# The load of the first superblock's gates waits for block 30 of the first expert product

## The chip, the core and the metric

The kernel runs on one core of a Trainium2 chip. The metric is the time of one execution on the device in microseconds (us); the kernel before was timed three times. One further execution was recorded by the profiler, and all rows below come from it. A core has TensorE (PE in the rows, PEld its weight loads), VectorE (DVE), ScalarE (ACT), GpSimd (POOL) and SyncE (SP); each executes its own instructions in order and waits on semaphores for the others.

## The reference

Two transformer blocks over 256 tokens of width 2048, in float32. The part that matters is the expert layer of the second block. Each token picks 16 of 16,384 experts in each of 8 heads; an expert is one row of `peer_u` and one of `peer_v`:

```python
def chunk(args):
    xc, ec, gc = args                     # tokens, chosen experts, their gates
    u = peer_u[ec]
    act = jax.nn.gelu(jnp.einsum('tkd,td->tk', u, xc))
    return jnp.einsum('tk,tkd->td', gc * act, peer_v[ec])
```

The gates are a softmax over the 16 best scores of a head. After this layer a gated projection and a last normalization follow.

## The kernel before

The kernel doesn't gather experts. It computes the layer densely, for all 16,384 of them: a first product of the tokens with all rows of `peer_u`, gelu, a multiply with a gate table that is zero where an expert was not chosen, and a second product with `peer_v`.

The table lies in DRAM as two arrays, `gate_table0` and `gate_table1`, one for each half of the tokens (128 each), experts by tokens. It is filled with zeros early in the program. The routing (`choose`) then adds each gate at its place: 256 indirect DMAs from GpSimd (line 1389, called scatters here), 128 single elements each, half of them into each table. The routing's steps run beside the products of later chunks.

The first product is cut into 32 blocks of 512 experts (`up(eb)`, blocks 0 to 31). A block is a tile of 128 partitions by 4 by 256 tokens. Its weights come in eight loads of 512 KB over SyncE's queue, called chunks here. The helper `wload` splits each chunk into a high part (`wh`, a cast on ScalarE, L217) and a low part (`wl`, a subtraction on VectorE, L218), with five buffers for the raw tiles, four for `wh`, three for `wl`. TensorE multiplies with both (L243 with `wh`, L245 with `wl`). `halves` adds the two accumulators of each bank (a copy on ScalarE, L280, an add on VectorE, L281), and gelu follows on ScalarE (L1421). Blocks 0 to 21 are written to DRAM (`spill`, line 1423); blocks 22 to 31 stay in SBUF in `hsb`.

The second product goes by superblocks of two blocks, first 11 to 15 (blocks 22 to 31, which are at hand), then 0 to 10. `weigh` does three things: it loads the gates into two tiles (line 1435, four loads of 128 x 4 x 128 elements: for each of two blocks one from each table), takes the blocks, and multiplies them with the gates on VectorE (L1445). The blocks are then split into high and low parts again (L301 on ScalarE, L302 on VectorE). `down` multiplies them with `peer_v` (L249 to L251) and adds the result to `hx` (L451). For all superblocks but the first one, `weigh` copies one element of `hx[0]` into the gates' tile ahead of the load (line 1433); the load of the first table overwrites that element and so waits for the copy.

All 32 blocks are called before the first `weigh` in the code. The order in which the instructions of an engine stand is set by a scheduler, which works with the dependences among tiles; the code's order is one of its inputs. The changed lines alone therefore don't tell where an instruction stands.

Of the kernel before, what the change touches and what calls it, by code (L numbers as in the profile page):

```python
# [133 lines left out]
class Kern:  # L134
# [1274 lines left out]
    def experts_(self, hx, xn, n5):  # L1409
        nc, i = self.nc, self.i  # L1410
        self.routing(xn)
        hsb, at = {}, {}
        SPILL, LAG = 11, 5
        spill = self.dramp.tile([2 * SPILL, P, 4, 256], F32, name="spill")
        xt = lambda k: xn.normal[k // 4](k % 4)

        def up(eb):
            banks = self.ws_chunk(xt, lambda kk: i["uT"][eb, kk // 2], KT, 512)
            b4 = self.blk()
            self.halves(b4, banks)  # L1420
            nc.scalar.activation(b4, b4, AF.Gelu_apprx_tanh)  # L1421
            if eb < 2 * SPILL:
                nc.scalar.dma_start(spill[eb], b4)
            else:
                hsb[eb] = b4

        def weigh(sb, first):
            g = []
            for u in range(2):
                gb = self.xp.tile([P, 4, 256], F32, name=self.nm("gates"), tag="gates")  # L1430
                if not first:

                    nc.gpsimd.tensor_copy(gb[:, 0, 0:1], hx[0][:, 0, 0:1])  # L1433
                for t in range(2):
                    nc.gpsimd.dma_start(gb[:, :, P * t:P * t + P], self.gd[t].rearrange("(i p) t -> p i t", p=P)  # L1435
                                        [:, 8 * sb + 4 * u:8 * sb + 4 * u + 4, :])
                g.append(gb)
            ap = []
            for u in range(2):
                if sb < SPILL:  # L1440
                    a = self.blk()
                    nc.gpsimd.dma_start(a, spill[2 * sb + u])
                else:
                    a = hsb.pop(2 * sb + u)
                nc.vector.tensor_tensor(a, a, g[u], OP.mult)  # L1445
                ap.append(Pair(self))
                ap[u].split(a)
            at[sb] = self.tiles_of(ap)

        def down(sb, last):  # L1450
            a = at.pop(sb)
            for j in range(4):
                banks = self.xs_chunk(a, lambda kk: self.wsrc(i["peer_v"], 8 * sb + kk, 512 * j, 512), 8, 512)
                self.add_rows(hx, j, banks)
                if last and j < 3:
                    n5.chunk(j, hx[j])


        order = list(range(SPILL, 16)) + list(range(SPILL))
        for n in range(SPILL + LAG):  # L1460
            up(2 * n)
            up(2 * n + 1)
        self.drain()
        for n, sb in enumerate(order):
            new = SPILL + LAG + n
            if new < 16:
                up(2 * new)
            weigh(sb, n == 0)
            if new < 16:
                up(2 * new + 1)  # L1470
            down(sb, n == 15)
# [195 lines left out]
```

## Time and profile before

| what | value |
|---|---|
| timed runs | 3850.2, 3848.3, 3850.9 us; median 3850.2 |
| profiled execution, device time | 3846.87 us |
| its span, first to last instruction | 3845.1 us |
| mean granted TensorE clock | 0.981 |
| TensorE busy | 3690.7 us (96% of the span) |
| VectorE, ScalarE, GpSimd busy | 63%, 49%, 18% |
| first and last scatter start | 2159.1 and 2827.0 us |
| first and last load of gates start | 2828.4 and 3656.4 us |

The profiled execution's device time lies 1.8 us above its span. In the rows, times are us from the start of the span. A row of a timeline gives start, duration, engine, line and operation, the tiles written and read, and how often it was merged; behind it, in brackets, how long the engine stood idle ahead of it and what released it. The order of an engine's instructions is the program's.

### The profile page before, as it was taken

How to read it: one execution, taken by the hardware profiler on the slowest of the kernel's cores; microseconds unless marked ns; L12 is line 12 of the kernel's file. 1: busy time of each engine (PE TensorE's matmuls, PEld its weight loads, DVE VectorE, ACT ScalarE, POOL GpSimd, SP SyncE). 2: the span in 40 equal slices, each digit the busy share in tenths (PEclk: the TensorE clock that was granted, in tenths of full speed). 3: DMA queues.
4: the chain of work that ended last, by engine and by line, in shares of the span. 5: the costliest groups of instructions: out<-in, count | busy, mean ns of one | idle time of the engine just before them, and what ended most of it. 6: DMA issues, size and time to landing. Idle time of an engine off the chain costs nothing.

```text
span 3845.1 us, 53526 instructions
## 1 busy us (share of the span) xinstructions
PE 3690.7 (96%) x19938; PEld 3163.1 (82%) x19938; DVE 2428.7 (63%) x4232; ACT 1867.3 (49%) x2586; POOL 691.6 (18%) x525
## 2 busy tenths in 40 slices
PE   9999989999999999999999999999249999999998
PEld 8888878888888898888888888888248888888887
DVE  7566667567576775578656998455124566666665
ACT  4344455455455555467645455444124444444455
POOL 0000030000000200001010366678730001111100
PEclk9999999999999999999999999999679999999999
DMA  6534486666666545666665678888346667777765
GB/s 221 150 112 148 137 329 189 195 191 186 195 192 189 163 133 169 194 185 183 179 196 182 182 207 212 211 212 212 48 112 188 200 212 234 249 242 240 237 205 162
DMA packets 368694, 728.82 MB, mean 190 GB/s; under 512 B 61072, under 2 KB 67696, under 8 KB 368432
## 3 DMA queue, kind: packets, MB, share of 16 engines
q1 hardware_dynamic: 311536, 658.19, 56.6%
q0 software_dynamic: 53296, 55.37, 6.4%
q10 hardware_dynamic: 3600, 11.83, 0.8%
q8 instruction: 156, 2.56, 0.3%
q14 instruction: 106, 0.87, 0.1%
HBM read 694.74 MB, written 30.54 MB: 189 GB/s over the span
## 4 chain that ended last, share of the span: by engine, by line
PE 73%; issue 10%; DMA 10%; POOL 4%; DVE 2%; ACT 1%; SPq 0%; DVEq 0%; ACTq 0%; POOLq 0%
PE acc L243 25%; PE acc L245 13%; PE acc L249 10%; PE acc L250 10%; PE acc L251 10%; DMA gate_table<-sm,sm 8%; POOL gate_table L1389 4%; PE ps L479 2%; DMA raw<-in_w_up_dram 1%; DVE wl L218 1%; PE ps L492 1%; DMA raw<-in_w_in_dram 1%; PE ps L1255 0%; PE ps L375 0%; POOL gates L1435 0%
## 5 line engine op out<-in xcount | busy, mean ns | idle before, releaser
L218 DVE TENSOR_TENSOR wl<-raw,wh 128x1024 fp32r<-128x1024 f32 x1249 | 1537.3, 1233 | 984.1 <-PE acc L245 527.1
L217 ACT CAST wh<-raw 128x1024 fp32r<-128x1024 f32 x1249 | 1300.1, 1045 | 1551.9 <-PE acc L243 721.9
L243 PE MATMUL acc<-b,wh 128*128 128x512 f32 x6128 | 1664.1, 397 | 6.6 <-DVE b L281 6.5
L243 PEld LDWEIGHTS acc<-b,wh 128*128 128x128 f32 x6128 | 1061.5, 189 | 163.7 <-DVE b L281 7.9
L245 PEld LDWEIGHTS acc<-b,wl 128*128 128x128 f32 x6128 | 920.4, 190 | 236.5 <-DVE wl L218 119.0
L245 PE MATMUL acc<-b,wl 128*128 128x256 f32 x6128 | 950.4, 282 | 118.2 <-DVE wl L218 118.2
L250 PE MATMUL acc<-wl,b 128*128 128x512 f32 (+1 forms) x1916 | 737.8, 385 | 3.1 <-DVE wl L218 3.0
L249 PE MATMUL acc<-wh,b 128*128 128x512 f32 (+1 forms) x1916 | 738.5, 386 | 0.0
L251 PE MATMUL acc<-wh,b 128*128 128x512 f32 (+1 forms) x1916 | 737.0, 385 | 0.0
L1389 POOL DMA_INDIRECT gate_table<-sm,sm x256 | 475.4, 1857 | 248.6 <-DMA gate_table<-sm,sm 150.0
L250 PEld LDWEIGHTS acc<-wl,b 128*128 128x128 f32 x1916 | 360.4, 188 | 75.6 <-DVE wl L218 6.0
L249 PEld LDWEIGHTS acc<-wh,b 128*128 128x128 f32 x1916 | 360.4, 188 | 74.2 <-issue 4.0
L251 PEld LDWEIGHTS acc<-wh,b 128*128 128x128 f32 x1916 | 360.4, 188 | 70.7 <-DVE b L302 0.3
L280 ACT COPY b<-acc 128x256 f32<-128x256 f32 x398 | 145.6, 371 | 120.1 <-PE acc L245 106.6
L281 DVE TENSOR_TENSOR b<-acc,b 128x256 f32<-128x256 f32 x398 | 164.8, 420 | 42.4 <-ACT b L280 41.3
L451 DVE TENSOR_TENSOR b<-b,acc 128x512 f32<-128x512 f32 x176 | 120.3, 684 | 64.0 <-PE acc L251 63.8
L1445 DVE TENSOR_TENSOR b<-b,gates 128x1024 f32<-128x1024 f32 x32 | 38.8, 1223 | 189.4 <-DMA gates<-gate_table 186.5
L1433 POOL COPY gates<-b 128x1 f32<-128x1 f32 x30 | 18.5, 648 | 750.7 <-DVE b L451 750.7
L954 POOL TENSOR_TENSOR b<-b,b 128x1024 f32<-128x1024 f32 x8 | 19.2, 2406 | 561.7 <-ACT b L953 387.6
L301 ACT CAST b<-b 128x1024 fp32r<-128x1024 f32 (+1 forms) x63 | 58.6, 942 | 125.7 <-DVE b L1445 92.0
L484 ACT ACTIVATE p<-sp,sm 128x128 f32<-128x128 f32 x120 | 53.9, 450 | 74.8 <-DVE sm L483 74.8
L302 DVE TENSOR_TENSOR b<-b,b 128x1024 fp32r<-128x1024 f32 (+1 forms) x63 | 67.9, 1086 | 22.9 <-ACT b L301 22.5
(315 smaller groups left out, 1849.7 us busy)
## 6 DMA issues: line engine op xcount, KB each, us to landing
raw<-in_uT_dram SPq DMA_DIRECT2D x256, 512.0 KB
raw<-in_peer_v_dram SPq DMA_DIRECT2D x256, 512.0 KB
raw<-in_w_in_dram SPq DMA_DIRECT2D x224, 512.0 KB
raw<-in_w_up_dram SPq DMA_DIRECT2D x176, 512.0 KB
raw<-in_w_down_dram SPq DMA_DIRECT2D x88, 512.0 KB
raw<-in_w_out_dram SPq DMA_DIRECT2D x64, 512.0 KB
gate_table<-sm POOLq DMA_DIRECT2D x64, 256.0 KB
raw<-in_w_attn_o_dram SPq DMA_DIRECT2D x32, 512.0 KB
```

The costliest lines, as they stand in the source:

```text
L217: nc.scalar.copy(h[:, :, :n], raw[:, :, :n])
L218: nc.vector.tensor_tensor(lo[:, :, :n], raw[:, :, :n], h.bitcast(F32)[:, :, :n], OP.subtract)
L243: mm(o.rearrange("p (a t) -> p a t", a=2), wh, x[2], start=start and d == 0, stop=False)
L245: mm(o[:, :256], wl, x[0], start=False, stop=stop and d == 1)
L249: mm(o, xh, wh, start=start, stop=False)
L250: mm(o, xh, wl, start=False, stop=False)
L251: mm(o, xl, wh, start=False, stop=stop)
L280: self.nc.scalar.copy(o, bank[:m, 256:])
L281: self.nc.vector.tensor_tensor(o, bank[:m, :256], o, OP.add)
L451: self.nc.vector.tensor_tensor(hx[j][:, t, :], hx[j][:, t, :], banks[t], OP.add)
L479: nc.tensor.matmul(s[:, c], q[a][:, qc], k[a][:, kc], start=a == 0, stop=a == len(q) - 1)
L1389: nc.gpsimd.indirect_dma_start(self.gd[t].rearrange("e (t o) -> (e t) o", o=1), bass.IndirectOffsetOnAxis(ap=at[:, t, k:k + 1], axis=0), g ...
```

## The change

The copy into the gates' tile is now made for the first superblock too. There its source is one element of block 30, the last block but one of the first product, where it is `hx[0]` for the others.

```diff
             for u in range(2):
                 gb = self.xp.tile([P, 4, 256], F32, name=self.nm("gates"), tag="gates")
-                if not first:
-
-                    nc.gpsimd.tensor_copy(gb[:, 0, 0:1], hx[0][:, 0, 0:1])
+
+                nc.gpsimd.tensor_copy(gb[:, 0, 0:1], (hsb[30] if first else hx[0])[:, 0, 0:1])
                 for t in range(2):
                     nc.gpsimd.dma_start(gb[:, :, P * t:P * t + P], self.gd[t].rearrange("(i p) t -> p i t", p=P)
                                         [:, 8 * sb + 4 * u:8 * sb + 4 * u + 4, :])
```

The lines behind it have numbers lower by one in the changed kernel (1432 for the copy, 1434 for the load, 1444 for the multiply). TensorE, ScalarE and SyncE keep their order; VectorE and GpSimd don't.

VectorE before, where the last adds of block 22 stand (`b_4463` is block 22, `gates_27359` its gates, `wl` low parts of the weights):

```order
L281 TENSOR_TENSOR b_4463_25639<-acc_25461,b_4463_25639 128x256
L218 TENSOR_TENSOR wl_25700<-raw_25697,wh_25699 128x1024
L281 TENSOR_TENSOR b_4463_25639<-acc_25462,b_4463_25639 128x256
L1445 TENSOR_TENSOR b_4463_25639<-b_4463_25639,gates_27359 128x1024
L218 TENSOR_TENSOR wl_25722<-raw_25719,wh_25721 128x1024
L218 TENSOR_TENSOR wl_25744<-raw_25741,wh_25743 128x1024
```

The multiply of block 22 stood right behind the block's last add; that of block 23 stood likewise behind block 23.

VectorE now, eight blocks later, behind the last adds of block 30 (`b_4695`); `b_4492` is block 23, and `wl_27242` to `wl_27330` are chunks 4 to 8 of block 31:

```order
L281 TENSOR_TENSOR b_4695_27159<-acc_26982,b_4695_27159 128x256
L218 TENSOR_TENSOR wl_27242<-raw_27239,wh_27241 128x1024
L218 TENSOR_TENSOR wl_27264<-raw_27261,wh_27263 128x1024
L1444 TENSOR_TENSOR b_4463_25639<-b_4463_25639,gates_27359 128x1024
L1444 TENSOR_TENSOR b_4492_25829<-b_4492_25829,gates_27363 128x1024
L218 TENSOR_TENSOR wl_27286<-raw_27283,wh_27285 128x1024
L218 TENSOR_TENSOR wl_27308<-raw_27305,wh_27307 128x1024
L218 TENSOR_TENSOR wl_27330<-raw_27327,wh_27329 128x1024
```

Both multiplies of the first superblock now stand between chunks 5 and 6 of block 31.

GpSimd before, from the last two scatters on (`gate_table_4891` is the table of the first token half, `gate_table_4892` that of the second, `b_687` is `hx[0]`):

```order
L1389 DMA gate_table_4891<-sm_19089,sm_19091 2097152x1
L1389 DMA gate_table_4892<-sm_19089,sm_19091 2097152x1
L1435 DMA gates_27359<-gate_table_4891 128x4x128
L1435 DMA gates_27359<-gate_table_4892 128x4x128
L1435 DMA gates_27362<-gate_table_4891 128x4x128
L1435 DMA gates_27362<-gate_table_4892 128x4x128
L1435 DMA gates_27679<-gate_table_4892 128x4x128
```

GpSimd now, at the same place:

```order
L1389 DMA gate_table_4891<-sm_19089,sm_19091 2097152x1
L1389 DMA gate_table_4892<-sm_19089,sm_19091 2097152x1
L1434 DMA gates_27359<-gate_table_4892 128x4x128
L1432 COPY gates_27359<-b_4695_27159 128x1
L1432 COPY gates_27363<-b_4695_27159 128x1
L1434 DMA gates_27363<-gate_table_4892 128x4x128
L1434 DMA gates_27359<-gate_table_4891 128x4x128
L1434 DMA gates_27363<-gate_table_4891 128x4x128
L1434 DMA gates_27681<-gate_table_4892 128x4x128
```

Two copies came in behind the first load, and three of the four loads stand behind them; the scatters stay ahead of all.

## Rows read from the trace of the kernel before

**Rows 1.** Timeline of TensorE around its longest wait.
```profile
2717.09 2.00 PE L243 MATMUL acc<-b,wh 128*128 128x512 f32 x8
...
2836.26 2.08 PE L245 MATMUL acc<-b,wl 128*128 128x256 f32 x8 [117.17 <-DVE wl L218]
2838.13 3.62 PE L243 MATMUL acc<-b,wh 128*128 128x512 f32 x8
...
2842.76 1.99 PE L243 MATMUL acc<-b,wh 128*128 128x512 f32 x8
...
2845.55 2.00 PE L243 MATMUL acc<-b,wh 128*128 128x512 f32 x8
```

**Rows 2.** TensorE's waits, whole span: us in total, times, longest.
```profile
PE acc L245 <- DVE wl L218: 118.2, 2, 117.2
```

**Rows 3.** Timeline of VectorE at block 22's end.
```profile
2710.09 0.42 DVE L281 TENSOR_TENSOR b<-acc,b 128x256 f32<-128x256 f32 x1
...
2833.84 1.23 DVE L1445 TENSOR_TENSOR b<-b,gates 128x1024 f32<-128x1024 f32 x1 [123.33 <-DMA gates<-gate_table]
```

**Rows 4.** Timeline of GpSimd, scatters and first loads.
```profile
2709.45 2.15 POOL L1389 DMA_INDIRECT gate_table<-sm,sm  x1 [0.62 <-DMA gate_table<-sm,sm]
...
2827.04 1.55 POOL L1389 DMA_INDIRECT gate_table<-sm,sm  x1 [0.30 <-issue]
...
2830.37 3.03 POOL L1435 DMA_DIRECT2D gates<-gate_table  x4 [0.93 <-DMA gate_table<-sm,sm]
```

**Rows 5.** Scatters by stretch: length, GpSimd busy (count), PEclk, DMA share, GB/s.
```profile
2159.00:2219.00 60.00, 43.68 (x23) 1.00 0.73 190
2219.00:2500.00 281.00, 175.32 (x96) 1.00 0.81 209
2400.00:2450.00 50.00, 29.64 (x16) 1.00 0.85 221
2500.00:2715.00 215.00, 162.08 (x77) 1.00 0.80 210
2718.00:2828.00 110.00, 91.95 (x60) 0.52 0.22 0
```

**Rows 6.** Chain that ended last: start, length from a scatter's issue to its landing.
```profile
2664.46 7.18 DMA gate_table<-sm,sm
...
2709.45 6.18 DMA gate_table<-sm,sm
...
2827.04 3.04 DMA gate_table<-sm,sm
```

**Rows 7.** The spill tile's writes: count, durations in ns, first and last start.
```profile
L1423 ACTq DMA_DIRECT2D spill<-b x22: 326/326/353, 2216.3 to 2689.3; - x22
```

**Rows 8.** Timeline of ScalarE: block 30's gelu, first cast for the second product.
```profile
3009.29 1.06 ACT L1421 ACTIVATE b<-b 128x1024 f32<-128x1024 f32 x1 [0.55 <-DVE b L281]
...
3028.17 1.05 ACT L301 CAST b<-b 128x1024 fp32r<-128x1024 f32 x1
```

**Rows 9.** Timeline of VectorE: chunks 5, 6 of block 31; second superblock's multiplies.
```profile
3013.30 1.22 DVE L218 TENSOR_TENSOR wl<-raw,wh 128x1024 fp32r<-128x1024 f32 x1 [1.62 <-PE acc L245]
3016.09 1.23 DVE L218 TENSOR_TENSOR wl<-raw,wh 128x1024 fp32r<-128x1024 f32 x1 [1.57 <-PE acc L245]
...
3049.66 2.36 DVE L1445 TENSOR_TENSOR b<-b,gates 128x1024 f32<-128x1024 f32 x2 [4.82 <-DMA gates<-gate_table]
```

**Rows 10.** Timeline of TensorE: chunk 6 of block 31, low part.
```profile
3023.26 1.11 PE L245 MATMUL acc<-b,wl 128*128 128x256 f32 x8
```

**Rows 11.** Timeline of GpSimd: the second superblock's copies.
```profile
3041.14 1.24 POOL L1433 COPY gates<-b 128x1 f32<-128x1 f32 x2 [207.74 <-DVE b L451]
```

**Rows 12.** TensorE's waits from 2860 to 3700 us.
```profile
PE acc L250 <- DVE wl L218: 1.6, 2, 1.1
```

**Rows 13.** VectorE's waits from 2860 to 3700 us, one of them.
```profile
DVE b L1445 <- DMA gates<-gate_table: 63.1, 15, 4.8
```

**Rows 14.** A stretch: PE, PEld, DVE, ACT, POOL busy (count), PEclk, DMA, GB/s.
```profile
2500.00:2700.00 200.00, 200.00 (x1148) 175.60 (x1147) 100.71 (x108) 96.08 (x117) 151.59 (x72) 1.00 0.81 213
```

## The prediction

> **What bounds the kernel now.** I read the page's forty slices first: TensorE's are full but for those around 2,720 to 2,840 us. So the table of TensorE's waits comes next: one wait of 117.2 us stands far above all others, and the releaser named is VectorE's subtraction L218, which makes the low half of a weight tile [rows 2]. The subtraction itself is short, so the question is what held VectorE. Its timeline shows it: the multiply L1445, `b <- b, gates`, starts at 2833.84 after 123.33 us of idleness, released by the load of the gates [rows 3]. The loads in turn stand on GpSimd behind the scatters L1389: the last scatter starts at 2827.04, and four loads are issued at 2830.37 [rows 4]. While VectorE stood, 60 scatters went through in the 110 us from 2718 to 2828, 1.85 us apart, with the granted clock at 0.52 [rows 5].
>
> That is a wait in the wrong place. The last piece of block 22 is added at 2710.09 [rows 3], but the weighted block is first read at 3028.17, by the cast that prepares the second product [rows 8]; nine more blocks of the first product (23 to 31) are still to come, and TensorE could do them while the scatters run. VectorE executes in order, so the early multiply holds every later L218, and some chunks later TensorE has no low halves left. Before the stall, with scatters and products side by side, TensorE is busy 200 of 200 us at clock 1.00 [rows 14]: scatters do not slow it.
>
> **The change part by part.**
>
> *The multiplies move.* In the changed order the two multiplies of the first superblock stand after the fifth weight subtraction of block 31, instead of one behind block 22 and one behind block 23. Their number and size are the same, so nothing is saved or added on VectorE but the place of the wait. What goes is the stall with its tail. The chunk that began at 2717.09 is followed by chunks at 2838.13, 2842.76 and 2845.55; the last two are one period apart, 2.79 us [rows 1]. Without the stall the third of them would start at 2717.09 + 3 x 2.79 = 2725.46. So the stall costs 2845.55 - 2725.46 = 120.1 us: 117.2 of idleness [rows 2], and 2.9 from matmul groups that ran long afterwards (3.62 us for eight that otherwise take 2.00 [rows 1]), while the granted clock was coming back from its lower level. This is the gain if nothing else is late. All times of before that lie after the stall I move forward by 120.1 us.
>
> *The two copies and the four loads.* GpSimd now executes: one load of the second token half, which the copy doesn't touch; two one-element copies, which wait for block 30's activation; three loads, and the prefetch for the next superblock. Block 30's activation starts at 3009.29 and takes 1.06 [rows 8], so 2890.3 after the shift. The nearest row for copy, loads and landing is the second superblock, which has the same sequence: copies at 3041.14 [rows 11], the first multiply at 3049.66 [rows 9], so 8.5 us. The first multiply would start at 2890.3 + 8.5 = 2898.8.
>
> *What waits behind it.* On VectorE the next instruction is the subtraction for chunk 6 of block 31. Without the multiplies ahead it would start at 3016.09 - 120.1 = 2896.0, its predecessor ends at 3013.30 + 1.22 - 120.1 = 2894.4 [rows 9]; TensorE uses its result at 3023.26 - 120.1 = 2903.2 [rows 10]. Two multiplies (2.36 us) and one subtraction (1.22) must fit ahead of that: the first multiply may start up to 2903.2 - 3.5 = 2899.7. With 2898.8 there are 0.9 us to spare, so VectorE stands 4.4 us and TensorE doesn't. The rows of the other 15 superblocks say the same: VectorE stood 63.1 us in 15 such waits [rows 13], and TensorE lost 1.6 us in all over that stretch [rows 12]. I cost this step at 0.1 us; if the cover is gone, each microsecond by which the multiply passes 2899.7 is a microsecond of TensorE.
>
> *The scatters now end later, and that is the unknown.* In before, the stall itself let them run fast. At 2710 the 194th of 256 starts (2709.45 [rows 4]), 62 are left, and now they run beside the products. The pace with products: 2.61 us (23 in 60 us) up to the first spill write, 2.93 (96 in 281 us) and 2.79 (77 in 215 us) with the spill writes, and 3.125 (16 in 50 us) in the slowest piece [rows 5]. The spill writes end with block 21, the last is issued at 2689.3 [rows 7], so the stretch to come is like the first, and I take 2.61. A loaded scatter lands 6.2 us after its start, at most 7.2 in the chain [rows 6]. Last landing: 2709.45 + 62 x 2.61 + 6.2 = 2877.5, before the 2890.3 of block 30, so the copy's wait ends last and hides the scatters. At 2.79 it is 2888.6, still hidden. At 2.93 it is 2897.3; the load that stands ahead of the copies then waits for it, 1.0 more than the 8.5 (four issues take 3.03 us [rows 4], one some 0.8), so 9.5 in all, and the multiply starts at 2906.8: 7.1 us lost. At 3.125 it is 2909.4 and 19.2 us lost. From below: nothing is won by faster scatters, since block 30 ends last; no gain beyond 120.1 from this step. I take 0 and keep 0 to 19.2.
>
> Here the Trainium skill, SBUF — State Buffer, section "SBUF: two separate sides", speaks against the change: DMAs of the GpSimd queue need descriptors that GpSimd writes, and VectorE's two-port work locks it out, so that a DMA of 620 ns took 3,100. Scaled to a scatter that would be an estimated 9.25 us instead of 1.85, 20 scatters by the time VectorE stops at the multiply, 42 left, and some 88 us of the gain given back. The trace agrees in part: GpSimd's busy time per scatter is 2.10 us (162.08 / 77) beside the products and 1.53 (91.95 / 60) without [rows 5], a factor of 1.4 and not 5.
>
> *Sum.* The profiled execution took 3846.9 us: 3846.9 - 120.1 + 0.1 = 3726.9. It lies 3.3 us below the median of the timed runs, 3850.2, and I expect the same offset afterwards: 3730.
>
> **The rivals.**
>
> *A. The scatters are late by a little.* Place: the load of row one on GpSimd, multiply at chunk 6 of block 31. For it: 2.93 and 3.125 are both in the trace. Against: both lie where the spill writes were, and the pace without them is 2.61. Time: 3730 + 7 to 3730 + 19, so 3737 to 3750.
>
> *B. Most of the scatters are starved beside VectorE.* This is the mechanism of the page named above, at its factor of five: from 2709.45 to 2894.4 (VectorE stops at the multiply) 185 us hold 20 scatters; 42 remain and then run 1.85 us apart, 77.7 us; landing 3.04 [rows 6] and the 9.5 us of load and copies put the multiply at 2984.6, 84.9 us late, plus 2.9 for the clock: 3730 + 88 = 3818. Against: 77 scatters in 215 us of products.
>
> *C. Slower than before.* The same place and the same wait, but the scatters don't get on at all while VectorE and the weight loads run. With n left at 2894.4, the loss is 1.85 n + 3.04 + 9.5 - 5.3 + 2.9; it passes the 120.1 us won from n = 60 on, so only if at most two of the 62 went through in 185 us. With all 62 left it is 124.8: 3855. It cannot be worse by much, since the stall itself sets the scatters free. The row of 77 in 215 us speaks against it.
>
> *D. The change doesn't do what it says.* The copy touches only the first token half's element, and one load of the second half stands ahead of it on GpSimd; if a multiply still stood early, VectorE would be held as before: 3850. Against: both multiplies, which need both halves, stand after the fifth subtraction of block 31 in the changed order.
>
> **How the numbers follow.** Forecast (nothing to 3 us lost): 0.74. A: 0.17. Something between A and B, an unforeseen later transfer in block 31 that takes 20 to 90 us: 0.03, with B in it. D, with all cases that end within 0.2% (7.7 us, about what a measurement of this kernel can tell from no change): 0.03. C, with whatever else ends on that side: 0.03. The predicted time is 3730. The range holds the forecast and A: from 3724 (the offset of the profiled run and the scatter of the timed ones, some 3 us, on top of the sum at no loss) to 3750 (the slowest pace). Faster 0.94, same 0.03, slower 0.03.
>
> **What the profile of the changed kernel would show.** TensorE without a break from 2700 to 2900 at clock 1.00, and block 30's activation near 2889 instead of 3009. The last scatter starting near 2871 and not before 2860: the pace beside the products continues, about 2.6 us apart, instead of 1.85. GpSimd then standing some microseconds, its copies released by the activation L1421 (right) or its load by a scatter (A). The first multiply near 2899, with VectorE idle about 4 us before it, and TensorE's waits for L218 there under 1 us. The prediction is wrong if TensorE stands in block 31 for more than some 20 us, if the multiply starts near 2834 with a long wait, or if a wait of comparable length turns up behind it that the present trace doesn't show.

## The result and the profile after

The changed kernel took 3731.25 us (median of four runs, 3728.06 to 3739.26) beside 3849.25 us before: a ratio of 0.97, with a 95% interval of 0.9679 to 0.972. The profiled execution has a span of 3726.3 us; before it was 3845.1.

The forty slices of the page show it at a glance. The first row is TensorE's busy share in tenths, the second GpSimd's, the third the granted clock:

```profile
PE   9999989999999999999999999999999999999998
POOL 0000030000000110001101056667677101111100
PEclk9999999999999999999999999999999999999999
```

The hole around 2,720 to 2,840 us is gone, from TensorE's row and from the clock's. GpSimd's scatters now fill one slice more. TensorE's wait at L245 for L218, 117.2 us long in [rows 2], is down to 0.9. Its largest group of waits now comes to 7.9 us, and its longest single wait, 4.8 us, stood in the profile before too (us in total, times, longest):

```profile
PE acc L243 <- DVE b L281: 7.9, 7, 3.9
PE ps L347 <- DVE mid L344: 6.7, 2, 4.8
...
PE acc L245 <- DVE wl L218: 0.9, 1, 0.9
```

The stretch in which TensorE stood before, by engine (columns as in [rows 14]):

```profile
2718.00:2828.00 110.00, 110.00 (x633) 96.61 (x632) 55.36 (x60) 53.45 (x65) 82.90 (x40) 1.00 0.75 189
```

TensorE works 110 of 110 us at full granted clock, and 40 scatters go through beside it where 60 went through in the stall [rows 5].

What moved to block 31 is seen on four engines. ScalarE's timeline: block 30's gelu, which answers to [rows 8].

```profile
2890.55 1.06 ACT L1421 ACTIVATE b<-b 128x1024 f32<-128x1024 f32 x1 [0.55 <-DVE b L281]
```

GpSimd's timeline, from the last scatter on, which answers to [rows 4, 11]:

```profile
2883.78 2.26 POOL L1389 DMA_INDIRECT gate_table<-sm,sm  x1 [0.54 <-DMA gate_table<-sm,sm]
2889.49 0.84 POOL L1434 DMA_DIRECT2D gates<-gate_table  x1 [3.44 <-DMA gate_table<-sm,sm]
2891.68 1.30 POOL L1432 COPY gates<-b 128x1 f32<-128x1 f32 x2 [1.36 <-ACT b L1421]
2892.92 3.02 POOL L1434 DMA_DIRECT2D gates<-gate_table  x4
```

VectorE's timeline around the two multiplies, which answers to [rows 3, 9]:

```profile
2894.56 1.23 DVE L218 TENSOR_TENSOR wl<-raw,wh 128x1024 fp32r<-128x1024 f32 x1 [1.62 <-PE acc L245]
2901.13 2.36 DVE L1444 TENSOR_TENSOR b<-b,gates 128x1024 f32<-128x1024 f32 x2 [5.35 <-DMA gates<-gate_table]
2903.41 4.63 DVE L218 TENSOR_TENSOR wl<-raw,wh 128x1024 fp32r<-128x1024 f32 x4
```

And TensorE's, chunks 6 and 7 of block 31, which answers to [rows 10]:

```profile
2902.68 2.00 PE L243 MATMUL acc<-b,wh 128*128 128x512 f32 x8
2904.68 1.21 PE L245 MATMUL acc<-b,wl 128*128 128x256 f32 x8
2905.73 2.00 PE L243 MATMUL acc<-b,wh 128*128 128x512 f32 x8
```

The wait is still there: VectorE stands 5.35 us. But it is short, and the low parts made ahead cover it: chunks 6 and 7 start 3.05 us apart instead of 2.79, so TensorE loses 0.3 us. The load of the second token half waited for the last scatter until 2889.49, the copies then 1.36 us for the gelu: scatters and block 30 end almost together.

### The profile page after: what moved, and what is told of

Its sections match the earlier page's. It is cut to its first block, busy times and chain, and to the rows that moved or that the text cites. A ratio compares the mean times of both kernels' runs of the same rounds, so it can differ in the third digit from the quotient of the medians.

```text
span 3726.3 us, 53533 instructions
## 1 busy us (share of the span) xinstructions
PE 3686.9 (99%) x19938; PEld 3159.0 (85%) x19938; DVE 2428.1 (65%) x4232; ACT 1867.0 (50%) x2586; POOL 723.8 (19%) x527
## 4 chain that ended last, share of the span: by engine, by line
PE 74%; DMA 17%; issue 4%; DVE 2%; POOL 1%; ACT 1%; SPq 0%; DVEq 0%; ACTq 0%; POOLq 0%
PE acc L243 25%; DMA gate_table<-sm,sm 15%; PE acc L245 13%; PE acc L250 10%; PE acc L249 10%; PE acc L251 10%; PE ps L479 2%; POOL gate_table L1389 1%; DVE wl L218 1%; DMA raw<-in_w_up_dram 1%; PE ps L492 1%; PE ps L375 0%; PE ps L1255 0%; DMA raw<-in_w_in_dram 0%; DMA raw<-in_w_ple_gate_dram 0%
## 5 line engine op out<-in xcount | busy, mean ns | idle before, releaser
L218 DVE TENSOR_TENSOR wl<-raw,wh 128x1024 fp32r<-128x1024 f32 x1249 | 1537.8, 1234 | 984.4 <-PE acc L245 524.9
L245 PEld LDWEIGHTS acc<-b,wl 128*128 128x128 f32 x6128 | 919.8, 190 | 119.4 <-DVE wl L218 1.8
L245 PE MATMUL acc<-b,wl 128*128 128x256 f32 x6128 | 949.5, 282 | 0.9 <-DVE wl L218 0.9
L1389 POOL DMA_INDIRECT gate_table<-sm,sm x256 | 504.6, 1971 | 275.6 <-DMA gate_table<-sm,sm 203.6
```

The costliest lines, as they stand in the source:

```text
L218: nc.vector.tensor_tensor(lo[:, :, :n], raw[:, :, :n], h.bitcast(F32)[:, :, :n], OP.subtract)
L245: mm(o[:, :256], wl, x[0], start=False, stop=stop and d == 1)
L1389: nc.gpsimd.indirect_dma_start(self.gd[t].rearrange("e (t o) -> (e t) o", o=1), bass.IndirectOffsetOnAxis(ap=at[:, t, k:k + 1], axis=0), g ...
```

## The experiments

The text quoted ahead of each result is what was expected before the run. Each ratio is to the kernel before, timed in the same round; the kernel before itself took 3843 to 3854 us there, so ratios rather than times are compared across rounds.

**Half of the scatters, old order.** Is the stall the wait for the scatters' end, and nothing else? The edit is to the kernel before.

```diff
-            for k in range(16 * h, 16 * h + 16):
+            for k in range(16 * h, 16 * h + 8):
```

> The kernel before, with half of the scatters (8 of each head's 16 gates are left out, so the output lacks them). Theory: the stall is the wait for the scatters' end and nothing else. 128 scatters at 2.75 us end near 2515, long before the multiply behind block 22, so there is no stall with the old order either: about 3730 us. Rival (the early multiply waits for something else, or the loads of gates themselves are slow there): 3800 to 3850 us.

Measured: 3727.74 us (3724.12 to 3729.34), ratio 0.9669 (0.9653 to 0.9685). The last scatter started at 2540.99, not near 2515, and the first superblock's loads were issued from 2543 to 2550, early enough all the same. VectorE's timeline behind block 22 shows the multiply at its old place:

```profile
2712.73 0.42 DVE L281 TENSOR_TENSOR b<-acc,b 128x256 f32<-128x256 f32 x1
2714.28 1.23 DVE L1445 TENSOR_TENSOR b<-b,gates 128x1024 f32<-128x1024 f32 x1 [1.13 <-ACT b L1421]
```

The early place by itself makes VectorE wait 1.13 us, for the gelu, and TensorE hardly at all (0.9 us at L245 for L218 in the whole program); its price in the kernel before is the lateness of the scatters.

**The scatters of one token half alone, old order.** What sets their pace?

```diff
             for k in range(16 * h, 16 * h + 16):
-                for t in range(2):
+                for t in range(1):
```

> The kernel before, with the scatters of the first token half alone (128 scatters, all into one table; the second half's gates stay zero in the output). Theory: scatters into one table go one after the other, each waiting for the landing of the one before, and two tables give two such chains, so that the pace of 2.75 us is half of landing (5.4) plus 0.3. One table: 5.7 us each beside the products, 3.3 us in the stall; by 2711 some 97 are through, 31 are left, 103 us: a stall of about 100 us remains, time about 3836 us although half of the scatters are gone. Rival (GpSimd's own work for a scatter, slowed beside VectorE, sets the 2.75): the 128 end near 2515, no stall, about 3730 us.

Measured: 3818.54 us (3812.41 to 3824.3), ratio 0.9913 (0.9896 to 0.9929). With as many scatters as the kernel above, it is 91 us slower. The scatters by stretch (length, GpSimd busy and count, clock, DMA share, GB/s):

```profile
2219.00:2500.00 281.00, 91.30 (x51) 1.00 0.76 210
2500.00:2700.00 200.00, 69.07 (x37) 1.00 0.77 213
```

The pace beside the products is 200 / 37 = 5.4 us, about twice that of two tables. Each scatter waits for the one before it on its table. TensorE's wait was 82.0 us, and not 100, since the pace was 5.4 and not 5.7, so that 25 scatters were left at 2711 rather than 31. With one table GpSimd's own work, the rival, doesn't set the pace: it was busy 69.07 / 37 = 1.87 us per scatter and idle for the rest. That it plays no part with two tables doesn't follow from this run.

**The source four blocks earlier.**

```diff
-(hsb[30] if first else hx[0])
+(hsb[26] if first else hx[0])
```

> The changed kernel, with the copy's source four blocks earlier (block 26). Theory: VectorE stops at about 2806 in block 27, TensorE at about 2815, with some 25 scatters left, which then run 1.85 us apart; the last starts near 2861, the multiply near 2871, TensorE goes on near 2874. Lost 59 us and 3 us of clock: about 3792 us. Rival (the change won by having a copy at all, which orders the loads behind it, wherever its source is): 3731 us.

Measured: 3797.95 us (3786.62 to 3799.81), ratio 0.9844 (0.9826 to 0.9863). The multiply moved to block 27, and the old stall came back in part. VectorE's and TensorE's timelines:

```profile
2881.36 1.23 DVE L1444 TENSOR_TENSOR b<-b,gates 128x1024 f32<-128x1024 f32 x1 [73.11 <-DMA gates<-gate_table]
```

```profile
2885.38 2.08 PE L245 MATMUL acc<-b,wl 128*128 128x256 f32 x8 [68.23 <-DVE wl L218]
```

The wait is 9 us longer than expected because 31 scatters rather than 25 were left at 2815, the last one starting at 2872.37 and not near 2861. The rival (a copy as such is enough) is out: what counts is the block that it waits for.

**The source one block later.** The same line with `hsb[31]`.

> The changed kernel, with the copy's source one block later (block 31). Theory (the place of the two multiplies in VectorE's order sets what TensorE loses; each microsecond past the point at which the product is used is lost): block 31's gelu ends at 2914.4, the multiply starts 9.5 us later, at 2923.9, TensorE needs the weighted block at 2911.3 and goes on about 3.5 us after the multiply's start: some 15 us lost, time about 3746 us, with one wait of 12 to 18 us at the first second product. Rival (any late copy does, since the second product's weights can be prepared ahead): 3731 us.

Measured: 3741.04 us (3740.67 to 3742.53), ratio 0.9707 (0.9691 to 0.9724). TensorE's timeline at the start of the second product:

```profile
2911.06 0.40 PE L245 MATMUL acc<-b,wl 128*128 128x256 f32 x2
2921.32 0.79 PE L249 MATMUL acc<-wh,b 128*128 128x512 f32 x1 [9.87 <-ACT b L301]
```

It stood 9.9 us, short of the 12 to 18 expected: the multiply started 4.7 us after the copies (2918.97 and 2914.25) where I had counted 9.5. There is a latest block too. The ratio's interval overlaps that of the changed kernel, so it is the wait in the trace, and not the time, that shows the loss.

**The multiplies on GpSimd, no copies.** If the stall is VectorE's queue, it must go without any change to the loads. The edit is to the kernel before:

```diff
-                nc.vector.tensor_tensor(a, a, g[u], OP.mult)
+                (nc.gpsimd if first else nc.vector).tensor_tensor(a, a, g[u], OP.mult)
```

> The kernel before, without the added copies; the two multiplies of the first superblock run on GpSimd instead of VectorE. Theory (the stall consists of VectorE's queue standing behind a multiply that waits, not of the late gates): VectorE goes on at block 22, the scatters end near 2884 as in the changed kernel, the loads land near 2896, and two multiplies of 2.4 to 3.3 us on GpSimd end by about 2903, ahead of the first use near 2910. No stall: 3728 to 3735 us beside 3731 for the changed kernel. Rival (the loads' early place, without a copy ahead of them, costs something itself, or GpSimd's multiplies come too late): 3740 us and more.

Measured: 3733.53 us (3727.34 to 3737.39), ratio 0.9687 (0.9673 to 0.97). GpSimd's timeline:

```profile
2889.82 2.23 POOL L1389 DMA_INDIRECT gate_table<-sm,sm  x1 [0.54 <-DMA gate_table<-sm,sm]
...
2902.51 5.74 POOL L1445 TENSOR_TENSOR b<-b,gates 128x1024 f32<-128x1024 f32 x2 [3.59 <-DMA gates<-gate_table]
```

The gates come as late as ever, no copy holds anything, and the stall is gone: TensorE waited once at L245 for L218, 0.7 us. The multiplies ended at 2908.25, some 5 us later than expected, but the cast that reads them started at 2909.87. That isolates the cause: an in-order queue behind one waiting instruction.

**The changed kernel again, beside it.**

> The changed kernel once more, beside the one with the multiplies on GpSimd. All theories: 0.97 of before, some 3731 to 3736 us, with less than 2 us of TensorE's time lost in block 31. If the 5 us that VectorE stands there cost more than the trace of one execution shows, the GpSimd version is faster by that.

Measured: 3735.59 us (3726.0 to 3743.21), ratio 0.9687 (0.9671 to 0.9703), the same as with GpSimd's multiplies. But its profiled execution was its slowest run and missed the expectation of less than 2 us. GpSimd's and TensorE's timelines:

```profile
2901.95 1.54 POOL L1389 DMA_INDIRECT gate_table<-sm,sm  x1 [1.08 <-DMA gate_table<-sm,sm]
2905.30 0.84 POOL L1434 DMA_DIRECT2D gates<-gate_table  x1 [1.81 <-DMA gate_table<-sm,sm]
```

```profile
2915.10 2.08 PE L245 MATMUL acc<-b,wl 128*128 128x256 f32 x8 [8.94 <-DVE wl L218]
```

Here rival A came true: the last scatter landed 15.8 us later than in the first profile, and TensorE stood. The pace was not the reason. From 2718 on the scatters were 2.8 us apart in both profiles, but by then 189 of the 256 had started here, and 196 in the first profile.

**Half of the scatters in the changed kernel, and the changed kernel beside it.** Does this lateness explain the spread?

> The changed kernel with half of the scatters (8 of each head's 16 gates left out of the output). If the spread of the changed kernel's runs (3726 to 3743 us) and the 8.9 us that TensorE stood in block 31 in one profiled execution come from scatters that land after block 30's gelu, this one shows neither: the copies wait for the gelu alone, the multiply starts 8.5 to 9.5 us after it, all runs lie within some 5 us, near 3727 us. Rival (the spread comes from elsewhere, such as the weight loads): the same spread and median as the changed kernel beside it.

> The changed kernel, beside the one with half of the scatters. If late scatters cost it: a median some 4 to 8 us above that one's, a wider spread. Otherwise the same.

Measured, on another chip: 3729.15 us (3727.72 to 3730.33) with half of the scatters and 3726.5 us (3725.37 to 3729.81) for the changed kernel, ratios 0.9702 (0.9689 to 0.9715) and 0.9697 (0.9684 to 0.971). They are the same within their intervals, against my expectation of 4 to 8 us. In this profile of the changed kernel the load waited for the last scatter until 2889.86 and the multiply started at 2898.38, in time. So lateness cost one profiled execution about 11 us (8.9 of waiting, the rest in slower matmuls behind it) and this one nothing. That it makes up the whole spread of 3726 to 3743 us isn't shown; the executions here came from different chips.

No version was clearly faster than the changed kernel.

## Why the prediction was right

The forecast of 3730 stands against 3731.25, and its main step held: a stall of 120.1 us went with the early multiply. The two spans differ by 118.8 us. The missing 1.3 us were there before the changed place: block 22's last add starts at 2711.44 in the profile after and at 2710.09 in [rows 3].

*The stall.* The half-scatter kernel and the GpSimd multiplies take away one link each, the late gates and VectorE's queue, and each gives the full gain. Both links are needed, as the prediction had it.

*The wait moved and stayed covered.* I expected VectorE to stand 4.4 us with the multiply at 2898.8; it stood 5.35, with the multiply at 2901.13. Copies to multiply took 9.45 us, not the 8.5 of the second superblock, and the gelu was 1.4 us later. The deadline I had worked out, 2899.7, moves by the same 1.4 us to 2901.1, which the multiply just reached, and TensorE lost 0.3 us. That agrees.

*The scatters: mis-sized.* The step "the stretch to come is like the first, and I take 2.61" failed. The pace was 162 / 59 = 2.75 (columns as in [rows 5]):

```profile
2718.00:2880.00 162.00, 122.46 (x59) 1.00 0.76 189
```

The first 60 us were a poor model, and the end of the spill writes changed little (2.83 from 2500 to 2715: 76 in 215 us). So the last scatter started at 2883.78, not near 2871, its landing came near 2889.2, not 2877.5, and the slack up to the end of the gelu was some 2 us, not 13. The time came out right because 2.79 was just covered too, as the prediction had said.

That it was covered is in part luck. The prediction took the 62 scatters left at 2710 as given and put all the doubt into their pace. In the three profiles of the changed kernel it is the number left that differs: 62 in the first and third, 69 in the second, the one in which TensorE stood. Seven more at 2.8 us are 20 us, more than the slack. Of the 14 timed executions of the changed kernel three (3739.26, 3741.23 and 3743.21 us) lie in rival A's range; only the last has a trace that shows why.

The chain of waits shows what the pace was made of in the first profile (start, us):

```profile
2867.06 5.83 DMA gate_table<-sm,sm
2872.89 0.45 issue
2873.34 4.78 DMA gate_table<-sm,sm
2878.12 0.27 issue
2878.39 5.12 DMA gate_table<-sm,sm
```

Landing, issue, landing: two such chains, one per table, run side by side, and half of landing plus issue is the pace: (5.2 + 0.3) / 2 = 2.8. From 2718 on, 59 of the last 60 scatters waited for a landing. But this isn't the only limit at that pace. In the kernel with block 31 as source, 42 of the 60 that started from 2718 to 2885 waited for none: GpSimd itself was busy for 2.5 us with one and took up the next 0.3 us later (GpSimd's timeline):

```profile
2858.66 2.49 POOL L1389 DMA_INDIRECT gate_table<-sm,sm  x1 [0.30 <-issue]
2861.46 2.49 POOL L1389 DMA_INDIRECT gate_table<-sm,sm  x1 [0.30 <-issue]
```

These are 2.79 apart as well, and 2.79 is the period of TensorE's chunks [rows 1], to which VectorE's subtractions keep. In all five profiles in which scatters ran beside products up to 2880 the pace from 2718 on was 2.77 to 2.79. Whether it follows that period isn't shown: no run varied the period.

*Rivals B and C.* The Trainium skill's rule (SBUF — State Buffer, section "SBUF: two separate sides") on VectorE locking GpSimd out rests on a DMA beside a copy of VectorE in a two-port mode. What VectorE runs here beside the scatters is a subtraction of two tensors, so the factor of five was no price for it: GpSimd's work per scatter rose from 1.53 us in the stall to 2.08 (122.46 / 59) beside the products. That rise isn't hidden, as a landing counts from the scatter's start and contains GpSimd's work: 1.55 of 3.04 us in the stall, 2.15 of 6.18 beside the products [rows 4, 6].

*Rival D* fell with the order and the trace alike; the load that stands ahead of the copies did no harm, since it waited for the scatters anyway.

## What to carry to other kernels

When an engine's longest wait ends with a late transfer, look first at what stands behind the waiting instruction in the same queue: if the result isn't needed yet, moving the wait, by a dependence or to another engine, can be worth the whole stall, as it was here. Work out the point from which the moved wait is late again, on both sides: here one block later cost a wait of 9.9 us, and four blocks earlier one of 68.2. Take the rate of the late work from a stretch with the load it will run beside, as the stall itself let it run fast here (1.85 us against 2.75). And ask how far along that work is when the wait begins: here it differed by seven scatters between executions of one kernel.

## What the runs showed of the hardware

Two one-element copies on GpSimd took 1.30 us where VectorE's subtraction ran at the same time (2891.68 above) and 0.30 where VectorE stood. GpSimd's timeline of the kernel with block 31 as source:

```profile
2914.25 0.30 POOL L1432 COPY gates<-b 128x1 f32<-128x1 f32 x2 [15.86 <-ACT b L1421]
```

It goes the other way too. VectorE's subtraction L218, otherwise 1.22 us, took 2.62 beside GpSimd's multiplies:

```profile
2903.38 2.62 DVE L218 TENSOR_TENSOR wl<-raw,wh 128x1024 fp32r<-128x1024 f32 x1 [1.57 <-PE acc L245]
```

The section of the Trainium skill named above says that an operation of VectorE with two inputs in SBUF and one of GpSimd that reads SBUF exclude each other; these rows agree.

Behind TensorE's wait of 9.9 us in the kernel with block 31 as source, the granted clock was at its lower level (1.2 GHz): it is 0.50 from 2921 to 2928 us, and 1.00 again from 2929 on (columns as in [rows 14]).

```profile
2921.00:2928.00 7.00, 5.90 (x13) 4.21 (x14) 3.90 (x4) 1.32 (x2) 0.00 (x0) 0.50 0.00 0
2929.00:2936.00 7.00, 7.00 (x32) 5.78 (x31) 2.63 (x3) 2.19 (x3) 0.00 (x0) 1.00 0.51 154
```
